# A hybrid S5 / RG-LRU encoder block: the chunk matrices of the state-space branch built by GpSimd instead of VectorE

## The chip, the cores and the metric

The kernel runs on one core of a Trainium2 chip. The metric is device microseconds of one execution, from the median of several. In the rows, PE is TensorE's matmul stream, PEld its weight loads, DVE is VectorE, ACT is ScalarE, POOL is GpSimd and SP the engine that issues the DMAs. L495 is line 495 of the kernel. Each engine runs its own instructions strictly in the order in which they stand, and waits on semaphores for the others.

## What is computed

One encoder block over 1024 tokens of width 1024: a norm, an input projection to five parts, two recurrent branches, a merge, a SwiGLU layer, a gated per-layer embedding and a last norm. The change lies in the first branch, a complex diagonal state-space model (S5) with 64 groups of 16 channels and 64 states, run in both directions:

```
u = rms_norm(h, g_mix);  u_a, x_b, gate_b, merge_a, merge_b = split(u @ w_in)
for d in range(2):                      # forward, backward
    lam_bar = exp(lam * dt);  b_bar = (lam_bar - 1) / lam * b
    state_t = lam_bar * state_{t-1} + b_bar u_t        # per group, 64 complex states
    y_a += Re(c . state)
g_a = gelu(y_a + u_a * s5_d)
```

## The kernel before

**Tiling of the branch.** The tokens are cut into 128 chunks of 8. The 64 groups go in 16 half-batches of 4 groups by 2 directions. For each half-batch the kernel builds small matrices: `mt` takes the 8 tokens of a chunk to its contribution to the state, `mo` takes the state at a chunk's start to the 8 outputs. A scan over the 128 chunks carries the state.

**What the names are.** `s5_mats(hb)` loads the table `tb` of half-batch hb and calls `gen` twice, for `mo` and for `mt`. Each call makes two products of 128x1024 (L495, one into the result, one into the scratch tile `mu`) and adds them (L497). So a half-batch has six such instructions, and the 16 half-batches 96. TensorE then makes the kernel of the lags `pk` from `mo` and `mt` (L508, L511) and transposes `mt` into `pmi` (L528). ScalarE copies `pk` into `kt` (L514, L515) and `pmi` into `mi` (L530). `s5_front` multiplies the inputs `U` by `mi` into `pS` (L543) and rotates them (L556, L557, L561) into `bb`. `s5_mid` scans twice (L578, L602) with the decays `dzf`, with the carries between segments in between, and rotates back (swap `rosw` on ScalarE, L473 and L474; products L556, L557) into `X` (L606). `s5_out` multiplies by `mo` and `m0` into the outputs `py` (L617 to L619).

**Order.** `s5_step(hb)` emits mid(hb), then the matrices and the front of half-batch hb+2, then out(hb). Between the steps stand the remaining projections (L151, 48 matmuls each, one or two to a step). A scheduler puts the instructions of every engine in an order by priorities and its own estimate of times; at run time this order is fixed.

**Buffers that matter.** `mo` has three buffers, so `mo` of half-batch hb+3 can be written only when `py` of half-batch hb has read its own. `mt` and `mu` have one each, `X` two, `dzf` and `Y` one. GpSimd also writes the zeros of `dzf`, of the carries and of `X` (memsets at L572, L575 and L605), in the same queue.

```
        def gen(o1, o2, q1, q2, name):
            t = st5(name, 3 if name == "mo" else 1, [128, 8, 16, 8])
            u = st5("mu", 1, [128, 8, 16, 8])
```

Of the kernel before, what the change touches and what calls it, by code (L numbers as in the profile page):

```python
# [14 lines left out]
DRAM = bass.MemoryType.DRAM  # L15
# [14 lines left out]
D = 1024  # L30
# [6 lines left out]
# columns of one half-batch (4 groups, 2 directions) of the S5 tables  # L37
# [11 lines left out]
def block_kernel(tc, a, out):  # L49
# [27 lines left out]
    # ------------------------------------------------------------ constants  # L77
# [6 lines left out]
    # loads the one table that all of the first norm needs  # L84
# [4 lines left out]
    # keeps the tensor engine's clock up until the input is there  # L89
# [29 lines left out]
    # ------------------------------------------------------------ weights  # L119
# [3 lines left out]
    def split(st, shape, name):  # L123
        """the raw weights of a staging tile as an exact pair"""
        wh = wp.tile(shape, F32R, name=f"wh_{name}", tag="wh", bufs=WH)
        wl = wp.tile(shape, F32R, name=f"wl_{name}", tag="wl", bufs=WH)
        A.copy(wh, st)  # L127
        V.tensor_sub(wl, st, wh.bitcast(F32))
        return wh, wl

    def wload(src, name):
        """[kk*128, n] of DRAM -> split tiles [128, kk, n]"""
        with hp():
            kk, n = src.shape[0] // 128, src.shape[1]
            st = wstage([128, kk, n], name)
            dma(st, src.rearrange("(k p) n -> p k n", p=128))
            return split(st, [128, kk, n], name)

    def gemm(ps, w, xhs, xls, ns=(0, 1), ms=slice(0, 128), pn=None, k0=0, first=True, last=True,
             sub=slice(0, 512)):  # L140
        """accumulate w[:, :, ms]^T x over the k tiles, float32 by three passes"""
        wh, wl = w
        kk = len(xhs)
        tot = 3 * kk
        i = 0
        for k in range(kk):
            for ww, xx in ((wh, xhs[k]), (wh, xls[k]), (wl, xhs[k])):
                for n in ns:
                    q = n if pn is None else pn
                    xn = xx[n] if isinstance(xx, list) else xx[:, n * 512:(n + 1) * 512]  # L150
                    T.matmul(ps[:, q * 512:(q + 1) * 512][:, sub], ww[:, k0 + k, ms], xn[:, sub], start=(first and i == 0),  # L151
                             stop=(last and i == tot - 1))
                i += 1
# [14 lines left out]
    # ------------------------------------------------------------ norm 1  # L168
# [4 lines left out]
    def rstd_newton(y, sq, t):  # L173
        """y = sqrt(sq / D + eps) on entry, its refined inverse on exit"""
        V.reciprocal(y, y)
        V.tensor_scalar(t, sq, 1.0 / D, EPS, MUL, ADD)
        V.tensor_tensor(t, t, y, MUL)
        V.tensor_tensor(t, t, y, MUL)
        V.tensor_scalar(t, t, -0.5, 1.5, MUL, ADD)
        V.tensor_tensor(y, y, t, MUL)  # L180
# [11 lines left out]
    def transposed_half(h):  # L192
        """the tokens of one half, feature-major, times the gain as exact pairs"""
        cs = slice(h * 512, h * 512 + 512)
        ks = range(KT) if h == 0 else range(2)
        for k0 in range(0, KT, len(ks)):
            pt = [(psm if h == 0 and i % 2 else psb)("ptx") for i in range(len(ks) // 2)]
            for j in range(4):
                for k in ks:
                    T.transpose(pt[k // 2][:, (k % 2) * 512 + j * 128:(k % 2) * 512 + (j + 1) * 128],  # L200
                                xt[h * 4 + j][:, (k0 + k) * 128:(k0 + k + 1) * 128], ident)
            for k in ks:
                src = pt[k // 2][:, (k % 2) * 512:(k % 2) * 512 + 512]
                g = gmix[:, k0 + k:k0 + k + 1]
                A.activation(xh[k0 + k][:, cs], src, AF.Identity, scale=g)
                V.scalar_tensor_tensor(xl[k0 + k][:, cs], src, g, xh[k0 + k][:, cs].bitcast(F32), MUL, SUB)
# [10 lines left out]
    # per-feature vectors become columns: one transpose of their rows  # L217
# [23 lines left out]
    # ------------------------------------------------------------ accurate exp on small tables  # L241
    def exp_acc(y, x, t1, t2, ti):
        """y = exp(x); t1, t2 temporaries like x, ti an int32 one"""
        V.tensor_scalar(y, x, 88.0, -87.0, MIN, MAX)
        V.tensor_scalar(t1, y, 1.4426950408889634, MAGIC, MUL, ADD)
        V.tensor_scalar(t1, t1, MAGIC, None, SUB)
        V.scalar_tensor_tensor(y, t1, -0.693359375, y, MUL, ADD)
        V.scalar_tensor_tensor(y, t1, 2.12194440e-4, y, MUL, ADD)
        V.tensor_scalar(ti, t1, 8388608.0, 127.0 * 8388608.0, MUL, ADD)
        V.tensor_scalar(t2, y, 1.9875691500e-4, None, MUL)  # L250
        for c in (1.3981999507e-3, 8.3334519073e-3, 4.1665795894e-2, 1.6666665459e-1, 5.0000001201e-1):
            V.scalar_tensor_tensor(t2, t2, c, y, ADD, MUL)
        V.tensor_tensor(t2, t2, y, MUL)
        V.tensor_tensor(t2, t2, y, ADD)
        V.scalar_tensor_tensor(y, t2, 1.0, ti.bitcast(F32), ADD, MUL)

    # ------------------------------------------------------------ S5 tables, [(d g), p] first
# [9 lines left out]
    def s5_tables():  # L267
        """the tables of all groups, to DRAM; yields between its parts"""
# [9 lines left out]
        # expm1(a) = 2 T / (1 - T), T = tanh(a / 2)  # L278
# [51 lines left out]
        # f = (exp(lam dt) - 1) / lam  # L330
# [18 lines left out]
        # chunk rotations: e0[c0], e1[c1]  # L349
# [14 lines left out]
        def transposed(dups, name):  # L364
            """dup slots [(d g), 8, 128] -> psum tiles [128, 8, 128 (d g)]"""
# [59 lines left out]
        # the same times the decay of one chunk  # L425
# [6 lines left out]
        # decays  # L432
# [11 lines left out]
        # output matrices: rows (d g h), columns (re p | im p)  # L444
# [3 lines left out]
        for (s0, s1), o, nm in (((cr, ci), O_K1, "k1"), ((ci, cr), O_K2, "k2")):  # L448
            obs = [slot(f"tb_{nm}{hh}", shape=[128, 8, 2, 4, 16]) for hh in range(2)]
            dups = [dup((s0[:, q * 8:(q + 1) * 8], s1[:, q * 8:(q + 1) * 8]), 1.0, 1.0, nm) for q in range(2)]  # L450
            for d, ps in transposed(dups, nm):
                for hh in range(2):
                    # 8 tiles of 8 groups: tile t holds half-batches 2t, 2t+1
                    src = ps[:, hh * 4:hh * 4 + 4, :].rearrange("p t (b n) -> p (t b) n", b=2)
                    A.activation(obs[hh][:, :, d].rearrange("p b g h -> p b (g h)"), src, AF.Identity, scale=sgn)
# [5 lines left out]
    # direct term, [h, g]  # L461
# [7 lines left out]
    # ------------------------------------------------------------ S5, four groups at a time  # L469
# [9 lines left out]
    def s5_mats(hb):  # L479
# [11 lines left out]
        def gen(o1, o2, q1, q2, name):  # L491
            t = st5(name, 3 if name == "mo" else 1, [128, 8, 16, 8])
            u = st5("mu", 1, [128, 8, 16, 8])
            for dst, o, q in ((t, o1, q1), (u, o2, q2)):
                V.tensor_tensor(dst, v8(o).unsqueeze(2).to_broadcast([128, 8, 16, 8]),  # L495
                                v16(q).unsqueeze(3).to_broadcast([128, 8, 16, 8]), MUL)
            V.tensor_tensor(t, t, u, ADD)  # L497
# [4 lines left out]
        # kernel of the lags -7 .. 7 within a chunk, [h', lag, g, h]; columns 112: of a group hold lag 0  # L502
# [19 lines left out]
        # row (h', j) of the lags from j on  # L522
# [41 lines left out]
    def s5_mid(hb, st):  # L564
# [19 lines left out]
        # carries of the 16-chunk segments: (value | swapped value) times (cos | sin)  # L584
# [54 lines left out]
    # ------------------------------------------------------------ the rest of the input projection  # L639
# [5 lines left out]
    def inproj_parts(kind, f, parts=((0, 1),)):  # L645
        """yields after each part of the products"""
# [7 lines left out]
        with hp():  # L654
            o = ot(f"oi_{kind}{f}")
            if kind == "u":
                # tokens of a chunk in reversed order
# [16 lines left out]
    # ------------------------------------------------------------ RG-LRU  # L674
    # softplus(-a_logit) = max(-a_logit, 0) + log1p(exp(-|a_logit|)); log1p(e) = 2 atanh(e / (2 + e))
# [46 lines left out]
    def lru_head(hd):  # L722
        xc, xch, xcl = lru_conv(hd)
        hf = [None, None]
        for d in range(2):
# [7 lines left out]
            for m in range(2):  # L733
# [6 lines left out]
                # y = 8 sp r;  a = exp(-y);  s = tanh(y / 2) = (1 - a) / (1 + a)  # L740
# [5 lines left out]
            for m in range(2):  # L746
                A.activation(tr[m], tr[m], AF.Exp, scale=spm8[:, cc[m]:cc[m] + 1])
                A.activation(tr[m], tr[m], AF.Identity, bias=ones[:, 0:1])
                # one Newton step for 2 / (1 + s) from 1 + exp(-y)
# [23 lines left out]
    # ------------------------------------------------------------ order of emission  # L773
# [33 lines left out]
    def load_split(src, k, name, scale, mk):  # L807
        """float32 rows of DRAM, scaled, as an exact pair"""
# [10 lines left out]
    def lru_step(share):  # L819
        """keeps the LRU at its share of its 16 steps"""  # L820
# [13 lines left out]
    # ------------------------------------------------------------ projections of the two branches  # L834
# [45 lines left out]
    def pair(name, dt=F32):  # L880
        """the two halves of the tokens"""
# [5 lines left out]
    def split_to(h, l, t, scale):  # L887
        """t * scale as exact pairs, half by half"""
# [20 lines left out]
    # ------------------------------------------------------------ w_o, residual, norm 2  # L909
# [4 lines left out]
    def rstd_half(n, acc):  # L914
        """1 / rms of the tokens of one half, on all partitions"""
# [13 lines left out]
    def gain(m, n, gname, vh, vl, acc):  # L929
        """the finished residual times its gain as an exact pair, and its squares"""  # L930
# [39 lines left out]
    # ------------------------------------------------------------ SwiGLU, hidden in blocks  # L970
# [3 lines left out]
    def hidden(ht, ns):  # L974
        """yields after each part of the products of one hidden tile"""
# [39 lines left out]
    # the last block by halves of the tokens, each with its norm; the per-layer embedding beside it  # L1015
# [46 lines left out]
    for n in range(2):  # L1062
# [3 lines left out]
        for m in range(8):  # L1066
# [9 lines left out]
            if m == 7 and n == 1:  # L1076
                # the table of the last norm, loaded ahead of it
# [9 lines left out]
        # final norm, token-major  # L1087
# [45 lines left out]
```

## Time and profile before

| what | value |
|---|---|
| median of 3 runs | 1987.41 us (1986.44 to 1988.29) |
| span of the profiled execution | 1986.9 us |
| TensorE busy, share of the span | 1914.5 us, 96% |
| VectorE busy | 1160.2 us, 58% |
| ScalarE busy | 845.4 us, 43% |
| GpSimd busy | 7.9 us |
| granted TensorE clock, mean | 0.988 |

The profiled execution's own time is its span, 1986.9 us; it lies 0.5 us under the median of the runs. The half-batches of the S5 branch run from about 154 to 512 us. A busy TensorE is modelled to the end of each matmul, so idle time is what tells whether it is held up. The shares over the whole span say little about this stretch, in which VectorE is far busier than on the mean.

### The profile page before, as it was taken

Reading aid. Unit: us, or ns where it says so; the run is one execution under the profiler, and the core shown is the slowest. Engines: PE = TensorE matmul, PEld = TensorE weight load, DVE = VectorE, ACT = ScalarE, POOL = GpSimd, SP = SyncE. Lnnn points to the kernel's source line nnn. Section 1 sums busy time; section 2 is a strip of 40 time slices with the busy share of each in tenths; the row PEclk is TensorE's granted clock in tenths of the full one; section 3 lists DMA queues with packets and bytes.
Section 4 is the critical chain, followed back from the end, with each engine's and each line's share of the span. In section 5 each row is a group of like instructions: output and inputs, shape, how many; then the busy total and the mean of one; then the engine's idle time right before and its main releaser. Section 6 shows DMA issues by size and latency. Waiting matters only on the chain.

```text
span 1986.9 us, 22847 instructions
## 1 busy us (share of the span) xinstructions
PE 1914.5 (96%) x9261; PEld 1587.3 (80%) x9261; DVE 1160.2 (58%) x1402; ACT 845.4 (43%) x1065; POOL 7.9 (0%) x60
## 2 busy tenths in 40 slices
PE   7999988999999999999999999999999999999998
PEld 6787777777787878788788888888888888888786
DVE  7518999998447587867445453333333334346576
ACT  6665666656465757574224321111111111114543
POOL 0000000000000000000000000000000000000000
PEclk9999999999999999999999999999999999999999
DMA  4794343433324364646544211111111111112232
GB/s 151 193 245 134 107 128 120 127 117 98 107 74 142 123 222 149 221 152 201 187 139 128 80 55 57 43 54 43 53 43 53 46 50 53 43 55 95 63 119 74
DMA packets 256682, 215.74 MB, mean 109 GB/s; under 512 B 30912, under 2 KB 228672, under 8 KB 256576
## 3 DMA queue, kind: packets, MB, share of 16 engines
q1 hardware_dynamic: 256576, 214.27, 34.9%
q8 instruction: 73, 1.20, 0.2%
q14 instruction: 33, 0.27, 0.0%
HBM read 160.70 MB, written 53.54 MB: 108 GB/s over the span
## 4 chain that ended last, share of the span: by engine, by line
PE 64%; DVE 4%; ACT 2%; issue 2%; DMA 2%; SPq 0%; DVEq 0%; ACTq 0%
PE pfd L151 12%; PE pfg L151 12%; PE pfu L151 12%; PE ppg L151 4%; PE pg L151 4%; PE pwo L151 4%; PE pbo L151 4%; PE pi_a L151 3%; PE pgl L151 2%; PE pao L151 2%; PE pi_b L151 2%; PE ppj L151 1%; DMA ld_yb<-ybd 1%; DMA xb<-xbd 1%; DVE lz L764 0%
## 5 line engine op out<-in xcount | busy, mean ns | idle before, releaser
L989 DVE TENSOR_TENSOR ft<-rstd,pfu 128x1024 f32<-128x1024 f32 x22 | 26.9, 1221 | 154.4 <-PE pfu L151 154.4
L1012 DVE TENSOR_TENSOR h<-h,pfd 128x1024 f32<-128x1024 f32 x40 | 48.7, 1221 | 111.1 <-PE pfd L151 111.1
L151 PE MATMUL pfu<-vh,wh_fu 128*128 128x512 f32 x352 | 111.5, 390 | 0.0
L151 PE MATMUL pfg<-vl,wh_fg 128*128 128x512 f32 x352 | 111.0, 389 | 0.0
L151 PE MATMUL pfg<-vh,wl_fg 128*128 128x512 f32 x352 | 111.0, 389 | 0.0
L151 PE MATMUL pfu<-vh,wl_fu 128*128 128x512 f32 x352 | 111.0, 389 | 0.0
L151 PE MATMUL pfg<-vh,wh_fg 128*128 128x512 f32 x352 | 111.0, 389 | 0.0
L151 PE MATMUL pfu<-vl,wh_fu 128*128 128x512 f32 x352 | 110.9, 389 | 0.0
L986 DVE TENSOR_TENSOR fg<-rstd,pfg 128x1024 f32<-128x1024 f32 x22 | 26.9, 1221 | 141.0 <-PE pfg L151 124.0
L127 ACT CAST wh_fg<-ws_fg 128x1024 fp32r<-128x1024 f32 x22 | 23.2, 1055 | 174.3 <-PE pfd L151 86.2
L127 ACT CAST wh_fu<-ws_fu 128x1024 fp32r<-128x1024 f32 x22 | 23.2, 1055 | 168.8 <-PE pfg L151 64.0
L151 PE MATMUL pfd<-fh,wh_fd 128*128 128x512 f32 x288 | 89.9, 391 | 0.0
L151 PE MATMUL pfd<-fl,wh_fd 128*128 128x512 f32 x288 | 88.9, 389 | 0.0
L151 PE MATMUL pfd<-fh,wl_fd 128*128 128x512 f32 x288 | 88.2, 389 | 0.0
L151 PEld LDWEIGHTS pfu<-vh,wh_fu 128*128 128x128 f32 x352 | 66.1, 188 | 14.1 <-ACT wh_fu L127 0.3
L151 PEld LDWEIGHTS pfu<-vl,wh_fu 128*128 128x128 f32 x352 | 66.1, 188 | 13.9 <-issue 0.2
L151 PEld LDWEIGHTS pfu<-vh,wl_fu 128*128 128x128 f32 x352 | 66.1, 188 | 13.8
L151 PEld LDWEIGHTS pfg<-vh,wh_fg 128*128 128x128 f32 x352 | 66.1, 188 | 13.7
L151 PEld LDWEIGHTS pfg<-vh,wl_fg 128*128 128x128 f32 x352 | 66.1, 188 | 13.7
L151 PEld LDWEIGHTS pfg<-vl,wh_fg 128*128 128x128 f32 x352 | 66.1, 188 | 13.7
L127 ACT CAST wh_fd<-ws_fd 128x1024 fp32r<-128x1024 f32 (+1 forms) x20 | 19.4, 968 | 126.6 <-PE pfu L151 68.2
L151 PEld LDWEIGHTS pfd<-fh,wh_fd 128*128 128x128 f32 x288 | 53.7, 188 | 12.6 <-ACT fh L890 1.7
(484 smaller groups left out, 4864.6 us busy)
## 6 DMA issues: line engine op xcount, KB each, us to landing
ws_fg<-in_w_ff_gate_dram SPq DMA_DIRECT2D x22, 512.0 KB, 3.7
ws_fu<-in_w_ff_up_dram SPq DMA_DIRECT2D x22, 512.0 KB, 3.7
ws_wo<-in_w_o_dram SPq DMA_DIRECT2D x16, 512.0 KB, 4.0
ws_fd<-in_w_ff_down_dram SPq DMA_DIRECT2D x16, 512.0 KB, 3.3
ws_pg<-in_w_ple_gate_dram SPq DMA_DIRECT2D x16, 512.0 KB, 3.9
tb<-tab SPq DMA_DIRECT2D x16, 384.0 KB, 3.1
rb<-tab SPq DMA_DIRECT2D x16, 264.0 KB, 5.6
x<-in_x_dram SPq DMA_DIRECT2D x8, 512.0 KB, 8.2
```

The costliest lines, as they stand in the source:

```text
L127: A.copy(wh, st)
L151: T.matmul(ps[:, q * 512:(q + 1) * 512][:, sub], ww[:, k0 + k, ms], xn[:, sub], start=(first and i == 0), stop=(last and i == tot - 1))
L986: V.tensor_tensor(g, rstd, pg, MUL)
L989: V.tensor_tensor(t, rstd, pu, MUL)
L1012: V.tensor_tensor(hres[m], hres[m], ps, ADD)
```

## The change

The three instructions in `gen` are issued by GpSimd (`G`) instead of VectorE (`V`); `tb`, `mo`, `mt` and `mu` lie in SBUF as before. The other lines of the diff are comments.

```
@@ gen
             for dst, o, q in ((t, o1, q1), (u, o2, q2)):
-                V.tensor_tensor(dst, v8(o).unsqueeze(2).to_broadcast([128, 8, 16, 8]),
+                G.tensor_tensor(dst, v8(o).unsqueeze(2).to_broadcast([128, 8, 16, 8]),
                                 v16(q).unsqueeze(3).to_broadcast([128, 8, 16, 8]), MUL)
-            V.tensor_tensor(t, t, u, ADD)
+            G.tensor_tensor(t, t, u, ADD)
             return t
```

The scheduler's order changes with it. Tiles carry numbers here: mo_2129, mt_2134 and pk_2139 are of half-batch 5, mo_2360 of 6; dzf_2097, rosw_2117 and X_2122 of 3, carry_2327 and X_2353 of 4.

On GpSimd, in the middle of the branch, one half-batch (a piece of the difference):

```order
+L495 TENSOR_TENSOR mu_2130<-tb_2125 128x1024
 L575 MEMSET carry_2327 128x8
 L572 MEMSET dzf_2097 128x64
+L495 TENSOR_TENSOR mt_2134<-tb_2125 128x1024
+L495 TENSOR_TENSOR mo_2129<-tb_2125 128x1024
 L605 MEMSET X_2353 128x8
+L497 TENSOR_TENSOR mo_2129<-mo_2129,mu_2130 128x1024
+L495 TENSOR_TENSOR mu_2135<-tb_2125 128x1024
+L497 TENSOR_TENSOR mt_2134<-mt_2134,mu_2135 128x1024
```

The six instructions now stand among GpSimd's three memsets; the product into `mo` (which waits for `py` of half-batch 2), the first sum, the second product into `mu` and the second sum stand behind one another.

On VectorE at the same place (a piece of the difference; carry_2096 and bb_1845 are of half-batch 3, and wl_in_x7 is the low part of a projection's weights):

```order
 L592 TENSOR_TENSOR carry_2096<-carry_2096 128x64
-L495 TENSOR_TENSOR mo_2129<-tb_2125 128x1024
 L594 SCALAR_TENSOR_TENSOR carry_2096<-carry_2096 128x64
-L497 TENSOR_TENSOR mo_2129<-mo_2129,mu_2130 128x1024
+L128 TENSOR_TENSOR wl_in_x7_2791<-ws_in_x7_2788,wh_in_x7_2790 128x1024
 L599 TENSOR_TENSOR carry_2096<-carry_2096,rb_1781 128x16x7
-L495 TENSOR_TENSOR mu_2135<-tb_2125 128x1024
 L600 TENSOR_TENSOR carry_2096<-carry_2096 128x8x7
-L497 TENSOR_TENSOR mt_2134<-mt_2134,mu_2135 128x1024
 L601 TENSOR_TENSOR bb_1845<-bb_1845,carry_2096 128x8x7
```

What filled VectorE's gaps between the short carry instructions is gone from there.

On ScalarE, around the copies that follow `pk` and `pmi` of half-batch 5, before:

```order
L473 COPY rosw_2117<-Y_2102 64x1024
L474 COPY rosw_2117<-Y_2102 64x1024
L514 COPY kt_2156<-pk_2139 16x64x7
L515 COPY kt_2156<-pk_2139 16x64x7
L530 COPY mi_2175<-pmi_2166 128x1024
```

and of the changed kernel:

```order
L514 COPY kt_2156<-pk_2139 16x64x7
L473 COPY rosw_2117<-Y_2102 64x1024
L474 COPY rosw_2117<-Y_2102 64x1024
L515 COPY kt_2156<-pk_2139 16x64x7
L530 COPY mi_2175<-pmi_2166 128x1024
```

Here the swap copies stand between the two `kt` copies; from half-batch 8 on they stand ahead of both, well before `pk`.

On TensorE the projections are dealt out anew. Between the `pk` of one half-batch and that of the next stand 47 to 50 matmuls of projections before (half-batches 3 to 15). Now it is 27 to 39 up to half-batch 9, 96 ahead of half-batches 10 and 14, and 48 ahead of 11, 12, 13 and 15. Behind the last `py` stand 45 more of them than before, between the last `pk` and the last `py` 96 instead of 114, and between the `pk` of half-batch 2 and the end of `py` of half-batch 0 there are 55.

## Rows read from the trace of the kernel before

**Rows 1.** Page: the span, and busy time of each engine.
```profile
span 1986.9 us, 22847 instructions
PE 1914.5 (96%) x9261; PEld 1587.3 (80%) x9261; DVE 1160.2 (58%) x1402; ACT 845.4 (43%) x1065; POOL 7.9 (0%) x60
```
**Rows 2.** Busy time by stretch (start:end, length, busy us and count of each engine).
```profile
153.97:465.89 311.92, 282.28 (x1880) 242.37 (x1878) 299.44 (x335) 194.74 (x270) 5.74 (x39) 0.99 0.39 119
```
**Rows 3.** TensorE's waits, 154 to 466 us (total, times, longest).
```profile
PE pS L543 <- ACT mi L530: 20.9, 13, 1.9
PE pk L508 <- DVE mt L497: 8.6, 10, 2.1
```
**Rows 4.** VectorE's groups, 153 to 466 us (busy, mean ns, idle before).
```profile
L495 DVE TENSOR_TENSOR mu<-tb 128x1024 f32<-128x1024 f32 x32 | 38.7, 1210 | 0.0
...
L497 DVE TENSOR_TENSOR mo<-mo,mu 128x1024 f32<-128x1024 f32 x16 | 19.1, 1197 | 0.0
```
**Rows 5.** TensorE's timeline, one step (start, duration, idle before it).
```profile
299.16 1.69 PE L508 MATMUL pk<-mo,mt 128*16 128x112 f32 x16 [0.97 <-DVE mt L497]
...
301.29 1.09 PE L528 MATMUL pmi<-ident,mt 128*128 128x128 f32 x8
302.13 0.48 PE L151 MATMUL pi_g<-xl,wh_in_g 128*128 128x512 f32 x1
...
306.32 2.05 PE L543 MATMUL pS<-U,mi 128*128 128x128 f32 x16 [1.64 <-ACT mi L530]
308.21 0.39 PE L617 MATMUL py<-U,m 128*128 128x128 f32 x2
...
311.04 0.70 PE L151 MATMUL pi_g<-xl,wh_in_g 128*128 128x512 f32 x2
...
319.73 1.69 PE L508 MATMUL pk<-mo,mt 128*16 128x112 f32 x16
```
**Rows 6.** VectorE's and GpSimd's timeline in the same step.
```profile
311.34 0.12 POOL L605 MEMSET X<- 128x8 f32 x1 [9.51 <-PE py L619]
...
314.27 1.21 DVE L495 TENSOR_TENSOR mo<-tb 128x1024 f32<-128x1024 f32 x1
...
318.36 1.22 DVE L497 TENSOR_TENSOR mt<-mt,mu 128x1024 f32<-128x1024 f32 x1
```
**Rows 7.** ScalarE's timeline in the same step.
```profile
301.53 1.05 ACT L473 COPY rosw<-Y 64x1024 f32<-64x1024 f32 x1 [2.04 <-DVE Y L602]
...
303.67 0.97 ACT L514 COPY kt<-pk 16x448 f32<-16x448 f32 x1
304.44 0.98 ACT L515 COPY kt<-pk 16x448 f32<-16x448 f32 x1
305.22 1.04 ACT L530 COPY mi<-pmi 128x1024 f32<-128x1024 f32 x1
```
**Rows 8.** GpSimd's timeline, its only instruction that reads SBUF and two memsets.
```profile
0.73 0.20 POOL masks.py:197 MEMSET ident<- 128x128 f32 x1 [0.29 <-POOLq L1122]
...
1.10 0.30 POOL masks.py:199 TENSOR_SCALAR_AFFINE_SELECT ident<-ident 128x128 f32<-128x128 f32 x1
1.34 0.10 POOL L83 MEMSET epsc<- 128x1 f32 x1
```
**Rows 9.** Timelines: the first product, and pk of half-batches 2, 3 and 15.
```profile
153.97 1.23 DVE L495 TENSOR_TENSOR mo<-tb 128x1024 f32<-128x1024 f32 x1 [2.75 <-DMA tb<-tab]
...
182.65 1.72 PE L508 MATMUL pk<-mo,mt 128*16 128x112 f32 x16
...
213.80 1.69 PE L508 MATMUL pk<-mo,mt 128*16 128x112 f32 x16 [0.65 <-DVE mt L497]
...
465.89 1.69 PE L508 MATMUL pk<-mo,mt 128*16 128x112 f32 x16
```
**Rows 10.** TensorE's timeline: first and last of 27 pairs of projection matmuls.
```profile
147.80 0.61 PE L151 MATMUL pi_x<-xh,wh_in_x 128*128 128x512 f32 x2
...
159.59 0.61 PE L151 MATMUL pi_x<-xh,wl_in_x 128*128 128x512 f32 x2
```

## The prediction

> **What bounds the kernel now.** I read the page first [rows 1]: TensorE is busy 1914.5 of 1986.9 us, so over the whole kernel there are only 72 us that it isn't. Then I read the stretch that the change touches, by its busy times [rows 2]. From the first product at 153.97 us to the last `pk` at 465.89 us VectorE is busy 299.4 of 311.9 us, 96%, and TensorE 282.3. So VectorE is full here, and yet the most that any relief of it can give back in this stretch is TensorE's idle time, 311.9 - 282.3 = 29.6 us. TensorE's waits [rows 3] say where that lies: 20.9 us at `pS` for the copy `mi`, and 8.6 us at `pk` for the sum into `mt`.
>
> Then I followed one step on three engines. `pk` starts at 299.16, the next at 319.73 [rows 5]: a step takes 20.57 us. Inside it runs a ring that no engine's share shows. `pk` and `pmi` lead to `mi` and `pS`, behind `pS` TensorE does `py`, and GpSimd's memset of `X`, which waits for the end of `py`, starts at 311.34 [rows 6]. That is 12.18 us after `pk`. The end of the same `py` also frees the buffer for the next `mo`. Four instructions then follow one another: product into `mo` (314.27), sum, product into `mu`, sum into `mt` (318.36, ends 319.58) [rows 6]. The next `pk` starts 0.15 us later. So a step is 12.18 us from `pk` to the end of `py`, and 8.39 us of VectorE from there to the next `pk`: four instructions of 1.2, some 3 us of other VectorE work ahead of them, and short ones between.
>
> **What is removed.** 96 instructions of 1.20 to 1.21 us [rows 4], 116 us of VectorE. None of it comes off the end by itself, since TensorE's order and the ring set the step.
>
> **What is added: the duration T of such an instruction on GpSimd.** The trace has none. Its nearest row is the affine select, which reads one operand of 128 columns in 0.30 us; a memset of one column takes 0.10 us, and one of 128 columns, which reads nothing, 0.20 us [rows 8]. That makes 0.20 / 128 = 1.56 ns a column for one operand that is read. For 1024 columns with one operand at that pace T = 0.10 + 1.60 = 1.7 us; with a second read at the same price it is 3.3. Below, VectorE's own 1.21 is a bound [rows 4], if GpSimd were as fast. I take 2.9 us: these instructions read two operands, so the upper row is the nearer, and a bit less since a product doesn't test an index for each column as the select does.
>
> The Trainium skill (GPSIMD Engine Reference, section 3, Performance versus the Vector engine) has 4497 ns for a sum of two operands of 2048 columns on GpSimd; half of it, 2.25 us, is an estimate, and no run here shows it yet. By that T the sum below would come to 2014 us.
>
> **The start.** VectorE builds three half-batches' matrices first. Now 18 instructions queue on GpSimd from 153.97 on [rows 9], so `pk` of half-batch 2 comes at 153.97 + 18 x 2.9 + 0.15 = 206.3 instead of 182.65. TensorE's order then has, up to the end of `py` of half-batch 0: `pk` and `pmi` 2.97 us, `pS` 1.89, `py` 2.83 [rows 5] and 55 projection matmuls at 0.2267 us (11.79 us for 52 of them [rows 10]), in sum 20.2. Then the four instructions, 4 x 2.9 + 0.25 (one memset and the hand-over): `pk` of half-batch 3 at 238.3 instead of 213.80 [rows 9].
>
> **The steps.** There are twelve from `pk` 3 to `pk` 15. A step is c + 0.25 + 4T, with c from `pk` to the end of `py`. Before, c is 12.18. Where ScalarE's swap copies stand between the `kt` copies, they cost 303.67 - 301.53 = 2.1 us between `pk` and `mi` [rows 7], and c stays near 12.0. Where they stand ahead of both, `mi` is ready after `pk` 2.13, two copies at 0.77, one of 1.04 and 0.2 of hand-overs, 4.9 us; `pS` and `py` follow, 4.7 with 0.3 for the wait: c = 9.9. With 13 projection matmuls before `pS` it is 11.0. By the order of the changed kernel c is 9.9 in four of the ten ordinary steps, 11.0 in three and 12.0 in three: mean 10.9. So an ordinary step is 10.9 + 0.25 + 11.6 = 22.75 us, and ten are 227.5. The two steps with 96 projection matmuls are bound by TensorE: 9.9 + 90 x 0.2267 = 30.3, together 60.6, with the four instructions covered. `pk` 15 then starts at 238.3 + 227.5 + 60.6 = 526.4 instead of 465.89: +60.5.
>
> **Behind it.** Between the last `pk` and the last `py` 18 fewer projection matmuls, -4.1 us; behind the last `py` 45 more, +10.2, in a part where TensorE is full. Sum: +60.5 + 6.1 = +66.6, so 1986.9 + 66.6 = 2053.5 us of span, and 0.5 more for the median: **2054 us**.
>
> What is hidden: the first product into `mu` and the one into `mt` (2T = 5.8) run while TensorE goes from `pk` to `py`. VectorE has room for its rest: 96% less 6 x 1.21 = 7.3 us a step leaves it 13 of 22.8 us. The new wait, of the product into `mo` for `py`, stands in GpSimd's queue ahead of `X`'s memset and the sums; `X` is needed by a later step, so only the sums are missed. The memset of `dzf` now stands behind a product; its scan comes several us later, after ScalarE's swap copies and the products behind them, so 2.9 us of delay do no harm. SP's order changes in a few places without a new wait that the ring would see.
>
> **The rivals.**
>
> *The two engines take turns at SBUF.* Nearly all that VectorE does here reads two SBUF operands (products, sums, scans), and so do the six instructions. No row shows both at it together; the memsets under a busy VectorE [rows 6] only write. If a GpSimd instruction first lets one of VectorE's finish, T grows by 1.21 us to 4.1. From the first rotation on that adds 4.8 to the start and 48.4 to the ten steps: 2054 + 53 = 2107 us. The point from which it decides is VectorE being busy in half of the four instructions' time. The Trainium skill states such a rule (SBUF — State Buffer, Who interferes with whom): a VectorE instruction with two SBUF inputs contends with a GpSimd instruction that reads SBUF, and the second one waits for the first; no row of before can show it.
>
> *GpSimd is quick and VectorE's relief counts.* With T = 1.7 the start is 184.7 + 20.2 + 7.05 = 212 (2 us early), the six light steps are 11.5 + 0.25 + 6.8 = 18.55, the four with 48 matmuls are 9.9 + 42 x 0.2267 = 19.4, and with 60.6 `pk` 15 comes at 461.5: -4.4 + 6.1, no change, 1989. With T = 1.21 the same sum gives 201.3 + 6 x 16.6 + 77.6 + 60.6 = 439.1, -26.8 + 6.1: 1967 us, faster. It decides from T under 1.6 us. For it speaks that VectorE is the full engine [rows 2], against it that T would have to be near the pace of one operand.
>
> *Partly shared.* T between 3.3 and 3.6 gives 2079 to 2097; that is the upper part of the forecast, not a case of its own.
>
> **How the numbers follow.** Forecast (T of 1.9 to 3.6, 1998 to 2097): 0.62. Turns: 0.17. Quick GpSimd: 0.16, two thirds of it faster. The rest, 0.05, is that the new order stalls on something I haven't seen. Each us of T is worth 18 + 4 + 40 = 62 us, so the bounds 1.7 and 3.3 alone give 1989 to 2079; with the turns the range that should hold 8 in 10 is 1992 to 2100. A measurement of this kernel can tell about 0.2% (4 us) from no change. Faster by more than that: 0.12; within it: 0.06; slower: 0.82.
>
> **What would show it.** In the changed kernel GpSimd's instructions take 2.2 to 3.3 us and stand back to back from the `X` memset to `pk`. `pk` waits for GpSimd's sum in nearly every ordinary step, 22 to 24 us apart, and TensorE's idle time in the stretch rises from 30 to near 95 us, most of it at `pk`. VectorE is at some 60% there, and its products and scans last as before (1.2 and 2.28 us). If these last longer, or GpSimd's instructions do only where VectorE is busy, the engines take turns. If TensorE still waits at `pS` and hardly at `pk`, GpSimd is quick. I am wrong if T is under 1.7 us, or if the four instructions don't stand on the way from `py` to `pk`.

## The result and the profile after

The changed kernel takes 2111.23 us (median of 4 runs, 2109.29 to 2112.77), the kernel before 1987.85 us in the same comparison (4 runs, 1986.44 to 1991.22). The ratio is 1.0617, 95% interval 1.0603 to 1.0631. The change costs 6.2%. The sign was forecast, the size was not: 2054 us was said, and 2111 lies 11 us above the upper end of the range.

The page of the changed kernel, span and busy times, against [rows 1]:

```profile
span 2110.4 us, 22805 instructions
PE 1943.6 (92%) x9261; PEld 1609.7 (76%) x9261; DVE 1169.6 (55%) x1306; ACT 848.1 (40%) x1067; POOL 243.3 (12%) x156
```

Two things in this line matter. VectorE lost 96 instructions, and yet is busy 9.4 us longer than before. Added up record by record over both traces, the 96 lasted 116 us, and the 1306 that it kept lasted 1118.7 us before and 1229.3 now: 111 us came onto them, all but 1 us of it onto instructions whose records overlap one of GpSimd's products or sums. (The busy time counts the small overlaps of neighbouring records once; by it 113 us came on.) And TensorE is busy 29.1 us longer for the same 9261 matmuls.

The stretch from 153.97 us to the last `pk`, which starts now at 585.72 instead of 465.89 (columns as in [rows 2]):

```profile
153.97:585.72 431.75, 305.36 (x1854) 259.42 (x1852) 316.54 (x246) 196.96 (x275) 241.46 (x137) 0.87 0.28 86
```

It is 119.8 us longer, so the loss of span (2110.4 - 1986.9 = 123.5 us) lies here but for 3.7. TensorE's idle time in it is 431.75 - 305.36 = 126.4 us instead of 29.6, and its granted clock 0.87 instead of 0.99. Its waits, 154 to 586 us, against [rows 3]:

```profile
PE pk L508 <- POOL mt L497: 72.8, 13, 10.6
PE pS L543 <- ACT mi L530: 48.5, 12, 12.5
```

The first wait was forecast. The growth of the second was not: it was 20.9 us before, and where the swap stands ahead the prediction had 0.3 us a step for it.

GpSimd's groups, 153 to 600 us, and VectorE's, 153 to 560 (busy us, mean ns of one, idle before):

```profile
L495 POOL TENSOR_TENSOR mu<-tb 128x1024 f32<-128x1024 f32 x32 | 77.6, 2424 | 2.2
L497 POOL TENSOR_TENSOR mo<-mo,mu 128x1024 f32<-128x1024 f32 x16 | 50.8, 3177 | 0.5
L497 POOL TENSOR_TENSOR mt<-mt,mu 128x1024 f32<-128x1024 f32 x16 | 41.6, 2599 | 1.3
L495 POOL TENSOR_TENSOR mo<-tb 128x1024 f32<-128x1024 f32 x16 | 35.3, 2206 | 127.7 <-PE py L619 115.2 <-DMA tb<-tab 12.5
L495 POOL TENSOR_TENSOR mt<-tb 128x1024 f32<-128x1024 f32 x16 | 32.3, 2021 | 12.9 <-PE pmi L528 12.9
```
```profile
L578 DVE TENSOR_TENSOR_SCAN Y<-dzf,bb 128x1024 f32<-128x1024 f32 x14 | 40.1, 2866 | 3.2 <-ACT dzf L573 1.6 <-ACT oi_x L661 0.5
...
L592 DVE TENSOR_TENSOR carry<-carry 128x64 f32<-128x64 f32 x14 | 28.0, 1999 | 0.2
L594 DVE TENSOR_TENSOR_SCAN carry<-carry 128x64 f32<-128x64 f32 x14 | 27.6, 1970 | 0.3
L556 DVE TENSOR_TENSOR risw<-risw,rb 128x1024 f32<-128x1024 f32 x14 | 22.5, 1609 | 27.2 <-ACT risw L474 27.2
...
L557 DVE TENSOR_TENSOR bb<-pS,rb 128x1024 f32<-128x1024 f32 x14 | 17.0, 1216 | 0.0
```

The same groups of the kernel before (153 to 466 us):

```profile
L578 DVE TENSOR_TENSOR_SCAN Y<-dzf,bb 128x1024 f32<-128x1024 f32 x14 | 31.9, 2279 | 0.4
...
L594 DVE TENSOR_TENSOR_SCAN carry<-carry 128x64 f32<-128x64 f32 x14 | 3.9, 276 | 0.0
...
L592 DVE TENSOR_TENSOR carry<-carry 128x64 f32<-128x64 f32 x14 | 3.0, 211 | 0.0
```

The two carry instructions of 64 columns, L592 and L594, took 0.21 and 0.28 us before and now take 2.0. The first scan grew from 2.28 to 2.87 us. The product that reads `pS`, which lies in PSUM (the memory that TensorE writes), kept its 1.21.

**What happens there** is seen in one step on both engines, GpSimd first (timelines, start and duration):

```profile
322.65 3.22 POOL L497 TENSOR_TENSOR mo<-mo,mu 128x1024 f32<-128x1024 f32 x1
325.95 2.82 POOL L495 TENSOR_TENSOR mu<-tb 128x1024 f32<-128x1024 f32 x1
328.84 3.40 POOL L497 TENSOR_TENSOR mt<-mt,mu 128x1024 f32<-128x1024 f32 x1
```
```profile
323.57 3.38 DVE L556 TENSOR_TENSOR risw<-risw,rb 128x1024 f32<-128x1024 f32 x1
326.88 1.21 DVE L557 TENSOR_TENSOR bb<-pS,rb 128x1024 f32<-128x1024 f32 x1
...
328.84 1.21 DVE L561 TENSOR_TENSOR bb<-bb,risw 128x1024 f32<-128x1024 f32 x1
329.97 2.35 DVE L592 TENSOR_TENSOR carry<-carry 128x64 f32<-128x64 f32 x1
```

Add start and duration. GpSimd's first sum ends at 325.87; L556 started while it ran and ends at 326.95, 1.08 us later, about its own 1.21. GpSimd's product was issued at 325.95 while L556 ran; it ends at 328.77, 1.82 after L556's end, about the 1.95 that such a product takes alone. GpSimd's next sum and L561 start together; VectorE's ends first, at 330.05, and the sum 2.19 us later, at 332.24. The carry L592 was issued at 329.97 and ends at 332.32: it stood behind the whole sum and then took its 0.21. Each instruction lasts until the other engine's has ended, and then its own time (less about 0.1 us, by which records of two instructions in a row overlap on one engine too). The engines take turns at whole instructions. The Trainium skill states this (SBUF — State Buffer, Who interferes with whom: the second port pair of VectorE is GpSimd's, and the lock on it is exclusive), and these rows agree. The turns need not alternate: in experiment 9 one of GpSimd's products (at 327.42) lasted 6.34 us, until four of VectorE's instructions had ended.

Alone, with VectorE idle, GpSimd's instructions take less than was forecast (timeline at the start):

```profile
157.01 1.96 POOL L495 TENSOR_TENSOR mu<-tb 128x1024 f32<-128x1024 f32 x1
...
160.84 2.34 POOL L497 TENSOR_TENSOR mo<-mo,mu 128x1024 f32<-128x1024 f32 x1
```

**A late step** shows where the second wait comes from. The first block is TensorE, the second ScalarE, the third VectorE (timelines):

```profile
456.10 1.72 PE L508 MATMUL pk<-mo,mt 128*16 128x112 f32 x16 [2.75 <-POOL mt L497]
...
468.81 3.79 PE L543 MATMUL pS<-U,mi 128*128 128x128 f32 x16 [8.07 <-ACT mi L530]
...
488.25 3.07 PE L508 MATMUL pk<-mo,mt 128*16 128x112 f32 x16 [2.33 <-POOL mt L497]
```
```profile
462.23 1.04 ACT L473 COPY rosw<-Y 64x1024 f32<-64x1024 f32 x1 [2.04 <-DVE Y L602]
...
466.20 0.92 ACT L514 COPY kt<-pk 16x448 f32<-16x448 f32 x1
466.93 0.97 ACT L515 COPY kt<-pk 16x448 f32<-16x448 f32 x1
467.71 1.05 ACT L530 COPY mi<-pmi 128x1024 f32<-128x1024 f32 x1
```
```profile
447.57 4.31 DVE L578 TENSOR_TENSOR_SCAN Y<-dzf,bb 128x1024 f32<-128x1024 f32 x1
...
453.81 2.32 DVE L592 TENSOR_TENSOR carry<-carry 128x64 f32<-128x64 f32 x1
456.16 2.06 DVE L594 TENSOR_TENSOR_SCAN carry<-carry 128x64 f32<-128x64 f32 x1
...
459.90 2.29 DVE L602 TENSOR_TENSOR_SCAN Y<-dzf,bb 128x1024 f32<-128x1024 f32 x1
```

The `pmi` of this half-batch is done by 459.4, but its copy `mi` stands on ScalarE behind the swap `rosw` of the half-batch before, and that waits for the second scan, which waits for the carries, which wait for the first scan. The first scan and the two carries of this step last 5.9 us longer than their 2.28, 0.21 and 0.28 of before. In the order of the changed kernel, up to `mi` of half-batch 9, the last swap ahead of a `mi` is that of two half-batches before; from `mi` of half-batch 10 on it is that of the half-batch just before. One half-batch of lead is gone, and what ran side by side is one chain: scan, carries, scan, swap, `kt`, `mi`, `pS`, rotation, scan. The three ordinary steps of this part take 35.6, 32.2 and 31.5 us.

**The clock.** Granted TensorE clock in three short windows of the same two steps (columns as in [rows 2]; the granted clock, as a share of 2.4 GHz, is the third number from the end):

```profile
306.25:309.40 3.15, 3.15 (x21) 2.50 (x22) 3.05 (x4) 0.24 (x1) 2.06 (x2) 0.50 0.00 0
...
456.10:457.90 1.80, 1.80 (x24) 1.80 (x25) 1.77 (x2) 0.00 (x0) 1.78 (x1) 1.00 0.00 0
468.80:472.40 3.60, 3.59 (x17) 3.59 (x18) 0.47 (x1) 0.84 (x1) 0.00 (x0) 0.50 0.93 281
```

After a wait of 6.2 us (at 306.25) and of 8.1 us (at 468.81) the clock is at its lower level, 1.2 GHz, and the same sixteen matmuls of `pk` take 3.18 us instead of 1.69, those of `pS` 3.79 instead of 2.05 [rows 5]. After 2.75 us of waiting (at 456.10) it is at 2.4 GHz, and `pk` takes 1.72. The length of the wait alone does not settle it: two `pk` came after 2.33 us of waiting, and the one at 488.25 took 3.07 us, the one at 519.72 took 1.72.

### The profile page after: what moved, and what is told of

Its sections match the earlier page's. It is cut to its first block, busy times and chain, and to the rows that moved or that the text cites. A ratio compares the mean times of both kernels' runs of the same rounds, so it can differ in the third digit from the quotient of the medians.

```text
span 2110.4 us, 22805 instructions
## 1 busy us (share of the span) xinstructions
PE 1943.6 (92%) x9261; PEld 1609.7 (76%) x9261; DVE 1169.6 (55%) x1306; ACT 848.1 (40%) x1067; POOL 243.3 (12%) x156
## 4 chain that ended last, share of the span: by engine, by line
PE 63%; DVE 5%; ACT 2%; issue 2%; DMA 1%; SPq 0%; DVEq 0%; ACTq 0%
PE pfd L151 11%; PE pfu L151 11%; PE pfg L151 11%; PE pg L151 4%; PE pwo L151 4%; PE ppg L151 4%; PE pi_b L151 4%; PE pbo L151 4%; PE pi_a L151 3%; PE pao L151 2%; PE pgl L151 1%; PE ppj L151 1%; DMA ld_yb<-ybd 1%; DVE lz L764 0%; DVE gg L768 0%
## 5 line engine op out<-in xcount | busy, mean ns | idle before, releaser
L508 PE MATMUL pk<-mo,mt 128*16 128x112 f32 x256 | 41.8, 341 | 75.0 <-POOL mt L497 72.8
L508 PEld LDWEIGHTS pk<-mo,mt 128*16 128x16 f32 x256 | 30.9, 130 | 86.9 <-POOL mt L497 78.3
L543 PE MATMUL pS<-U,mi 128*128 128x128 f32 x256 | 44.0, 343 | 55.6 <-ACT mi L530 55.0
L543 PEld LDWEIGHTS pS<-U,mi 128*128 128x128 f32 x256 | 40.7, 251 | 61.9 <-ACT mi L530 60.9
L495 POOL TENSOR_TENSOR mu<-tb 128x1024 f32<-128x1024 f32 x32 | 77.6, 2424 | 2.2
```

What stands on the lines that cost most here:

```text
L495: G.tensor_tensor(dst, v8(o).unsqueeze(2).to_broadcast([128, 8, 16, 8]), v16(q).unsqueeze(3).to_broadcast([128, 8, 16, 8]), MUL)
L508: T.matmul(pk[0:16, q * 128:q * 128 + 112], bq[q], mo[:, q, :, d:d + 7], start=True, stop=True)
L543: T.matmul(pS[:, q * 128:(q + 1) * 128], mi[:, q, :], rhs, start=True, stop=True)
```

## The experiments

Except in the last three, each kernel was run once, beside one run of the kernel before (1986.8 us for the first four, 1986.2 for the next ones). The echoes needed room for a scratch tile, so their control is the kernel before with one buffer for `mi` instead of two.

**1. The control.**

```
-MI = 2
+MI = 1
```

> The kernel before with one buffer for mi instead of two, which frees the room that the next three need for a scratch tile. Every theory expects 1985 to 1995 us: mi is written only after its last reader is done.

Measured 1981.79 us, a little faster than the kernel before and 3 us below the range that was expected (experiment 10 takes this up).

**2. The echo: GpSimd's work without its consequences.** VectorE still makes `mo` and `mt`; in each `gen` GpSimd makes two products and a sum as well, into a tile that nobody reads.

```
+            gt = st5("gt", 1, [128, 8, 16, 8])
+            for o, q in ((o1, q1), (o2, q2)):
+                G.tensor_tensor(gt, v8(o).unsqueeze(2).to_broadcast([128, 8, 16, 8]),
+                                v16(q).unsqueeze(3).to_broadcast([128, 8, 16, 8]), MUL)
+            G.tensor_tensor(gt, gt, gt, ADD)
```

> The control, and GpSimd also issues the six instructions of each half-batch (same operands, same shapes) into a scratch tile that nobody else reads. VectorE still does the work that counts. Theory A (VectorE and GpSimd take turns where both read SBUF with two operands): some 12 us of GpSimd's reads a half-batch are pushed between VectorE's, VectorE is 96% full, so +10 to +13 us a step, 2110 to 2170 us, and VectorE's products and scans last longer than 1.21 and 2.28 us. Theory B (no turns; GpSimd is only slower, and what waits for it pays): 1985 to 2000 us and VectorE's durations as before.

Measured 2127.93 us, 146 above the control. VectorE does the same 1402 instructions and is busy 1308.7 us, against 1161 to 1162 in the kernels with one buffer for `mi`: 147 more, as much as the whole loss, as theory A has it. (The scratch work also holds the table `tb` longer, so that GpSimd itself waits for loads; TensorE's largest wait is for VectorE's sum into `mt`, 107.4 us from 150 to 700 us.) One chain of turns in it, GpSimd first:

```profile
302.37 2.75 POOL L502 TENSOR_TENSOR gt<-gt 128x1024 f32<-128x1024 f32 x1
305.19 3.82 POOL L500 TENSOR_TENSOR gt<-tb 128x1024 f32<-128x1024 f32 x1
```
```profile
303.50 3.77 DVE L583 TENSOR_TENSOR_SCAN Y<-dzf,bb 128x1024 f32<-128x1024 f32 x1
307.18 2.91 DVE L561 TENSOR_TENSOR risw<-risw,rb 128x1024 f32<-128x1024 f32 x1
```

The sum ends at 305.12, the scan 2.15 later (2.28 alone), GpSimd's product 1.74 after that (1.95 alone), VectorE's product 1.08 after that (1.21 alone). So GpSimd's work costs VectorE time even where no other instruction reads its results.

**3. The echo with writes only.** Seven memsets of 128x1024 and one copy of eight columns in each `gen`.

```
+            G.tensor_copy(gt[:, 0, 0, :], tb[:, o1:o1 + 8])
+            for _ in range(7):
+                G.memset(gt, 0.0)
```

> The control with, in place of the echo, one copy of 8 columns and seven memsets of 128x1024 on GpSimd for each call of gen: about as much GpSimd time, but it only writes. Theory A, if the reads are what collides: 1985 to 2000 us and VectorE's durations as before. If writes collide too, or if the queue of GpSimd (the zeros of dzf and X behind the added work) is what costs: as slow as the echo.

Measured 1990.76 us. In the window from 180 to 470 us GpSimd is busy 226 of 290 us, more than in the echo (187), and VectorE's instructions keep their times (group, 180 to 480 us):

```profile
L582 DVE TENSOR_TENSOR_SCAN Y<-dzf,bb 128x1024 f32<-128x1024 f32 x15 | 34.2, 2281 | 4.0 <-POOL dzf L576 3.8
```

So a busy GpSimd alone costs little (9 us over the control); what it does with SBUF decides. Here it only wrote, but for the copies of eight columns.

**4. The echo with one operand.** Three copies of 128x1024 in each `gen`.

```
+            for o in (o1, o2, o1):
+                G.tensor_copy(gt, v8(o).unsqueeze(2).to_broadcast([128, 8, 16, 8]))
```

> The control with three copies of 128x1024 (one operand read from tb by the same broadcast) on GpSimd for each call of gen. Theory A: six copies a half-batch collide as well, each for its own duration, which I take at 1.0 to 1.7 us: +5 to +9 us a step, 2060 to 2130 us. If only two-operand instructions on GpSimd collide, or by theory B: 1985 to 2000 us.

Measured 2043.88 us: 62 over the control, between the two ranges that were named. It is less than theory A expected, but no longer harmless. VectorE's first scan takes 3.0 us. GpSimd's group, 180 to 480 us, and one copy that met no instruction of VectorE (timeline):

```profile
L500 POOL COPY gt<-tb 128x1024 f32<-128x1024 f32 x77 | 147.1, 1910 | 36.5 <-DMA tb<-tab 32.4
...
236.68 1.04 POOL L500 COPY gt<-tb 128x1024 f32<-128x1024 f32 x1 [1.03 <-DMA tb<-tab]
```

Alone a copy takes 1.04 us, about half of the product with two operands (1.95). The mean of 1.91 holds the waiting for VectorE's turns.

**5. The lead given back.** The changed kernel, with a higher priority for the matrices, so that the scheduler issues them earlier; the same in the first two half-batches.

```
-            sts[hb + 2] = {"m": s5_mats(hb + 2)}
+            with hp(400):
+                sts[hb + 2] = {"m": s5_mats(hb + 2)}
```

> The changed kernel with the matrices' code (s5_mats) emitted at a higher priority. In its order the copy mi of half-batch h+2 stands ahead of the swap of half-batch h+1 on ScalarE to the end, where the changed kernel loses that lead from half-batch 10 on. Theory C (of the 57 us beyond the forecast, most is the lost lead: from half-batch 10 on mi waits behind the swap of the half-batch just before it, so scan, swap, mi, pS, front and scan run in one chain): the late steps fall from 32 us to 24 to 27, 2070 to 2088 us. Rival D (the turns and the low clock of TensorE alone make the steps long): 2100 to 2115 us.

Measured 2091.64 us, 20 below the changed kernel and in neither of the two ranges, 4 us above that of theory C. The last `pk` starts at 565.26 instead of 585.72, and the late steps take 26.3 to 27.5 us instead of 31.5 to 35.6. The early ones, with the new order, take up to 27.3 us, where they took at most 26.3. So giving back the lead is worth about 20 us, net of what the new order costs elsewhere, and its theory goes no further than that. TensorE's waits (150 to 600 us) show what is left; the wait for `mi` is nearly gone, that for the sum has grown:

```profile
PE pk L508 <- POOL mt L497: 107.5, 16, 10.3
PE pS L543 <- ACT mi L530: 6.2, 5, 3.0
```

**6. The wait of the product into `mo` taken away,** by a fourth buffer (with one for `mi` to make room).

```
-MI = 2
+MI = 1
-            t = st5(name, 3 if name == "mo" else 1, [128, 8, 16, 8])
+            t = st5(name, 4 if name == "mo" else 1, [128, 8, 16, 8])
```

> The changed kernel with four buffers for mo and one for mi, so that the product into mo no longer waits for the py just done. Theory E (the ring from py over GpSimd's four instructions to the next pk sets the early steps): steps up to half-batch 9 fall from 25.4 to 20 to 23 us, and 2111 becomes 2080 to 2098 us; the late steps stay at 32. If the ring is not what binds there: 2105 to 2115 us.

Measured 2095.65 us. The total lies where it was expected, the reason does not hold: the early steps did not fall to 20 to 23 us (they are 25.1, 25.9, 22.2, 27.6), and the late ones, which were to stay at 32, are 30.6, 27.4 and 27.6. The gain lies in the late steps. The one buffer for `mi` was not run by itself in the changed kernel, so its share in this is not known. TensorE's waits, same window:

```profile
PE pS L543 <- ACT mi L530: 69.8, 12, 10.1
PE py L618 <- DVE X L606: 21.7, 6, 5.7
PE pk L508 <- POOL mt L497: 13.9, 2, 10.0
```

The wait at `pk` is nearly gone, and one for VectorE's chain stands in its place. The ring that the prediction was built on is not the only bound.

**7. Half of the change:** `mt` on GpSimd, `mo` on VectorE.

```
+            E = G if name == "mt" else V
-                G.tensor_tensor(dst, ...
+                E.tensor_tensor(dst, ...
-            G.tensor_tensor(t, t, u, ADD)
+            E.tensor_tensor(t, t, u, ADD)
```

> Half of the change: GpSimd builds mt (two products and a sum), VectorE still mo. Theory A with the ring: GpSimd's part from py to pk is two instructions of 2.9 us beside two of VectorE's at 1.2 to 2.3, about 9.5 us in place of 11.7, and half the turns: steps of 22 to 24 us, 2015 to 2055 us. If GpSimd's use as such cost something (its start, its queue) rather than its reads and its share of the ring: above 2070.

Measured 2052.98 us, +66.7, within the first range: half of the instructions bring 54% of the loss. A smaller share was not run.

**8. The kernel before with `kt` and `mi` earlier on ScalarE,** on top of the one buffer for `mi`.

```
+            with hp(200):
                 A.copy(mi.rearrange("p d n -> p (d n)"), pt)
```

(the same around the two `kt` copies)

> No GpSimd in it: the control of the first call (one buffer for mi) with the copies kt and mi at a higher priority on ScalarE, where TensorE waited 20.9 us in all for mi. If that wait is what keeps TensorE from being full in the stretch, 1965 to 1978 us; if the wait only moves to VectorE's sum ahead of pk (VectorE is full), 1980 to 1988.

Measured 1982.26 us, in the second range, and as with the one buffer alone.

**9. Both cures together,** edits 5 and 6.

> The changed kernel with both cures: the matrices' priority raised so that the order keeps its half-batch of lead, and four buffers for mo (one for mi). Alone they gave 2091.6 and 2095.7, 20 and 16 us below the changed kernel. If they take away different waits, the gains add: 2070 to 2080 us. If both only shorten the same chain, which VectorE's and TensorE's longer instructions then set: 2086 to 2098 us, with TensorE's wait at pk under 40 us in the stretch and its granted clock there still under 0.95. The theory that the order and the buffer make most of the loss gives under 2040.

Measured 2107.28 us (4 runs, 2104.04 to 2109.36), ratio 1.0604 [1.0590, 1.0618]. All three ranges were missed: the gains don't add, and together they are worse than either. The two signs of the second theory are there, TensorE's wait for the sum at `pk` is down to 16.2 us and the clock from 150 to 600 us is 0.85, but not its time. Its waits (same window):

```profile
PE py L618 <- DVE X L606: 47.4, 8, 9.1
PE pk L508 <- ACT g L621: 28.4, 4, 10.8
PE pk L508 <- POOL mt L497: 16.2, 3, 10.5
```

and VectorE's groups (153 to 560 us) why `X` is late:

```profile
L557 DVE TENSOR_TENSOR Y<-Y,rb 128x1024 f32<-128x1024 f32 x13 | 24.4, 1879 | 0.0
L606 DVE TENSOR_TENSOR X<-Y,rosw 128x1016 f32<-128x1016 f32 x13 | 24.3, 1869 | 0.2
```

These two took 1.22 and 1.20 us in the changed kernel. GpSimd, no longer held by `py`, now runs beside the rotation back, and VectorE's busy time over the whole run rises to 1183.8 us. The turns are not avoided by a better order; they fall on other instructions.

**10 and 11. Versions of the kernel before:** the one buffer for `mi`, and with it the earlier copies of experiment 8.

> The kernel before with one buffer for the copy mi instead of two, all products on VectorE. A single run gave 1981.79 beside 1986.81 of the kernel before. If the gain is real: ratio 0.996 to 0.999, 1980 to 1985 us. If it was scatter between executions: ratio 0.999 to 1.001.

> The same one buffer for mi, with ScalarE's copies kt and mi at a higher priority. A single run gave 1982.26 beside 1986.24 of the kernel before. If both edits add: ratio 0.995 to 0.997, below the kernel with the one buffer alone. If the priority only moves the wait: within 0.1% of the kernel with the one buffer alone.

1981.62 us (6 runs) and 1982.28 us (12 runs) beside 1987.43 (18 runs): ratios 0.9973 [0.9962, 0.9984] and 0.9976 [0.9968, 0.9985]. The one buffer gives 0.3%, the priority nothing more. Both are slightly faster than the two kernels of this case. Only TensorE's wait for `mi` was read to say why: over the whole run 22.6 us before and 12.5 with the one buffer. Why a smaller buffer gives an order with less of that wait was not tested.

## Why the prediction was right or wrong

What the forecast and the trace have between them is 2110.4 - 2053.5 = 56.9 us of span:

| part | forecast | measured | difference |
|---|---|---|---|
| `pk` of half-batch 3 starts at | 238.3 | 230.52 | -7.8 |
| ten ordinary steps | 227.5 | 278.4 | +50.9 |
| two steps with 96 projection matmuls | 60.6 | 76.8 | +16.2 |
| behind the last `pk`, against before | +6.1 | +3.7 | -2.4 |

The steps divide further at the start of the product into `mo`. Over the ten ordinary steps c, from `pk` to there, is 16.3 us on the mean instead of 10.9, 54.4 us in all, and the rest of a step 11.5 instead of 11.85, -3.5 in all. In the two long steps c is 18.1 and 19.3 instead of 9.9.

**T, right in the ring by luck.** In an early step the product into `mo` starts at 320.57 and the next `pk` at 332.30: 11.73 us, that is 0.25 + 4 x 2.87, and in the late step above, from the start of that product to `pk`, 488.25 - 476.45 = 11.80. The forecast was 2.9. But it was to be 2.9 as the work of one instruction by itself, from a price of 1.6 us for each operand that is read. Alone, a product takes 1.95 and a sum 2.34, a mean of (4 x 1.95 + 2 x 2.34) / 6 = 2.08 us for the six; a copy, with one operand, takes 1.04 (experiment 4). So the second operand does cost about as much as the first, as the prediction argued, but some 0.9 us each: the price taken from a row of 128 columns was too high. The rest up to 2.9 is the waiting for VectorE's turn, 3.18 for the sum into `mo`. The Trainium skill's figure (GPSIMD Engine Reference, section 3, Performance versus the Vector engine), from which 2.25 was estimated, is nearer to what the engine does alone. The sum by that T, 2014 us, is further from the result: with the right T and no turns the forecast would have been worse.

**The start, 7.8 us too long,** because most of its instructions run while VectorE is idle and take 1.95 and 2.34 us, not 2.9.

**The failed step is c, the time from `pk` to the end of `py`.** It was taken as 9.9 to 12.0 us. It is 14.3 in the early step (306.25 to 320.57, where the product into `mo` starts) and 20.4 in the late one (456.10 to 476.45). Behind c stood three things taken over from the trace of before, and each failed:

- "its products and scans last as before" (VectorE's instructions keep their times). They carry 111 us of waiting. The prediction looked for the turns in T alone, where they were priced at 1.21 us. GpSimd's 96 instructions carry only some 38 us of waiting (237.6 us in the groups above less 64 x 1.95 + 32 x 2.34 alone); most fell on VectorE, and there on the chain that feeds `X` and the swap. That turns alone can cost this much is shown by the echo, 146 us where VectorE still does the work that counts, and by the memsets, which cost 9.
- The swap out of the way (c of 9.9, where it stands ahead of both `kt` copies). That the swap stands ahead was read rightly from the order; that it would be done in time was not in the order. It waits for a chain that had got longer, and at half-batch 10 the order gives up one half-batch of lead. In the four ordinary steps that were to have this c (from half-batches 10, 11, 12 and 14) it is 23.4, 20.4, 19.7 and 14.2. Experiment 5 prices the lost lead at about 20 us.
- The durations of TensorE's own pieces. After the longer waits they ran at half the clock: `pk` 3.18 for 1.69, `pS` 3.79 for 2.05. Over the whole run this is the 29.1 us of added busy time. No run took the clock apart from the waits, so that is read from rows and not shown by an experiment, and how much of it lies on the path stays open.

**The two long steps** were to be bound by TensorE's 96 projection matmuls, 30.3 us each. They take 37.2 and 39.6. The `pk` behind them (420.51 and 559.32) start without a wait, so the four instructions were covered, as said; what is longer is c, with waits for `mi` of 3.4 and 8.1 us in it.

**Behind the last `pk`** the sum held: 3.7 for 6.1.

**The rivals.** *Turns at SBUF* was the right mechanism with the wrong price. Its 2107 us is near the result, but its T of 4.1 is nowhere to be seen; the time came out near by another way. It was given 0.17, though the prediction itself put VectorE at some 60% in the stretch, above the half from which it said that turns decide. What was open was only whether there are turns, which no row of before could show. *Quick GpSimd* fell: at 1.95 to 2.34 us alone, T is above its limit of 1.6.

**The signs named to look for.** "If these last longer, or GpSimd's instructions do only where VectorE is busy, the engines take turns" was the right test, and the trace answers yes to both halves. `pk` does wait for GpSimd's sum in nearly every step, 24 to 26 us apart early on (said: 22 to 24). TensorE's idle time is 126 us (said: 95), 72.8 of it at `pk`, VectorE's share 316.5 / 431.75 = 73% (said: 60%). The move of the memsets did no harm, as said: TensorE waits 2.3 us for `X` in the stretch, and the scan waits for `dzf` 1.6.

**What stays open** is the split of the remaining loss, after the lead is given back, between the turns on the chain and the lower clock. Experiment 9 shows only that it does not go away when the wait at `pk` does.

## What to carry to other kernels

Work that reads SBUF and is moved to GpSimd may come back onto VectorE where that reads two SBUF operands: here 116 us went and 111 came back. Price a moved instruction by its time on GpSimd, added to whichever of VectorE's instructions it meets, short ones on the chain above all. Ask of each duration copied from the old trace whether its engine will still run undisturbed, and whether TensorE will have waited before it. Where two engines can collide, measure it with an echo, the same work into a tile that nobody reads, before the path is rebuilt around it.

## What the runs showed of the hardware that was not expected

- A VectorE instruction of 64 columns takes 2.0 us instead of 0.21 when it is issued just behind the start of a GpSimd sum: it waits for the whole instruction, and is not merely slowed.
- VectorE's product with one operand in PSUM (L557 from `pS`) keeps 1.21 to 1.22 us beside GpSimd in every kernel here, and beside GpSimd's memsets, 954 ns for 128x1024, VectorE's instructions keep their times (first scan 2.28 us in experiment 3).
- GpSimd alone takes 1.04 us for a copy, 1.95 for a product, both with broadcast operands, and 2.34 for the sum of two full tiles. A copy of eight columns took 0.19 us at its shortest and 1.05 in the mean beside a busy VectorE (180 to 480 us of experiment 3); one of them (at 203.86) lasted 9.19, until seven of VectorE's instructions had gone ahead. A memset of eight took 0.11.
